# Filter features high over low on 128 partitions, and a differential head's values high beside low

## The chip, the cores and the metric

The kernel runs on one core of a Trainium2 chip. The metric is the device time of one execution in microseconds; the median of three runs stands for the kernel. The engines are TensorE (PE, with its weight loads as PEld), VectorE (DVE), ScalarE (ACT), GpSimd (POOL) and SyncE (SP), which issues most of the loads.

## The reference, cut to what matters

A residual stream of 256 tokens and 256 context tokens, 1024 wide, goes through a Hyena layer, an attention layer, and two trunk layers. Two places matter here. The first is the implicit filter of the Hyena layer, three sine layers of width 64 and a product with `w4`:

```python
    h = jnp.sin(fq * (z @ w1 + b1))
    h = jnp.sin(fq * (h @ w2 + b2))
    h = jnp.sin(fq * (h @ w3 + b3))
    h = h @ w4                       # (256, 2 * 2048)
    ...
    hf, hb = h[:, :E_HY] * decay, h[:, E_HY:] * decay
```

The second is the differential attention of the trunk layers, four heads of width 64 with two score maps each:

```python
    p = jax.nn.softmax(s, axis=-1)               # s: scores of the maps m = 0, 1
    a = p[:, :, 0] - lam * p[:, :, 1]
    return jnp.einsum('bhqk,bkhd->bqhd', a.astype(v.dtype), v)
```

The first trunk layer has 512 queries (256 of the context among them), the second 256.

## The kernel before, in words

Products are made in a rounded 32-bit form (`F32R`). To keep precision each factor is split into a high part and a low rest: `split` (L280) casts on ScalarE (L281) and subtracts on VectorE (L282). `mm3` (L284) then makes three matmuls, high by high, high by low, low by high (L285 to L287). Weights come by SP in blocks of 512 KB into five buffers and are split in the same way (`load_w`).

The filter. One load brings the weights of the sine layers, the positions `zt` and the biases (L493). Three sine layers follow on 64 partitions (L767 to L784): a matmul, the bias and the frequency (L776), a reduction of the argument (L778 to L782), the sine. Their result is split into `h3` (L787). `hy_filter` (L629) makes the filter of one of eight groups of 256 channels: it splits the group's `w4`, and for either parity of the positions one `mm3` with K = 64 gives 512 columns (L638), which VectorE multiplies by the decay (L640). The weights of group 0 are loaded by SP at the start, those of the others by ScalarE's queue (L624).

The differential attention. `keys` (L1145) splits the values into `vd`; `maps` (L1180) makes the scores of both maps, the exponentials and their weighted difference; `turn` transposes the result into `ats`; `values` (L1211) sums over the key tiles, two for the context queries and four for the others, with one `mm3` of 256 columns per tile. Its stationary operand is 128 columns wide, two heads, of which the unit uses one half: ScalarE copies that half to `od` (L1217). `attend` runs the three as a pipeline with lags. The sums and the transposes take turns in two PSUM banks (`tpps`, L262).

The order: in the first stage TensorE's instructions stand as written out (`START`, `manual_schedule`); elsewhere the order of each engine's instructions is worked out by the framework when the program is built. Each engine takes its instructions in order.

Of the kernel before, what the change touches and what calls it, by code (L numbers as in the profile page):

```python
# [15 lines left out]
F32 = mybir.dt.float32  # L16
# [6 lines left out]
P = 128  # L23
# [44 lines left out]
def _cols(v):  # L68

    return v.reshape(-1, P).T  # L70
# [10 lines left out]

def _vecs(i):

    z = [("ng0", _cols(i["norm_g"][0])), ("ab0", _cols(i["ada_b"][0])), ("ng1", _cols(i["norm_g"][1]))]
    for l in range(2):
        z += [(f"n1g{l}", _cols(i["norm1_g_2"][l])),
              (f"n2g{l}", _cols(i["norm2_g_2"][l]))]
    z.append(("fing", _cols(i["final_g_2"])))
    for l in range(2):
        z.append((f"ab{2 + l}", _cols(i["b_ada_2"][l])))  # L90
    z.append(("ab1", _cols(i["ada_b"][1])))
    for t in range(3):
        z.append((f"hcw{t}", _cols(i["hy_conv_w"][0, t])))
    z.append(("hcb", _cols(i["hy_conv_b"][0])))
    z.append(("hyd", _cols(i["hy_d"][0])))
    for l in range(2):
        for t in range(3):
            z.append((f"sc{l}{t}", _cols(i["sconv_w_2"][l, t])))
            z.append((f"fc{l}{t}", _cols(i["ffn_conv_w_2"][l, t])))
        z.append((f"sub{l}", np.tile(i["subln_g_2"][l], 2).reshape(P, 1)))  # L100
        for n in ("q1", "k1", "q2", "k2"):
            z.append((f"l{n}{l}", _rep(i[f"lambda_{n}_2"][l])))
    z += [("qg", _rep(i["at_q_g"][0])), ("kg", _rep(i["at_k_g"][0]))]
    off, o = {}, 0
    for n, v in z:
        off[n] = (o, v.shape[1])
        o += v.shape[1]
    return np.ascontiguousarray(np.concatenate([v for _, v in z], axis=1)), off
# [69 lines left out]
def _prep(i):  # L178
# [15 lines left out]

    A["ada3"] = np.ascontiguousarray(i["w_ada_2"][1].T.reshape(48, P, 1024))
    A["cbc"] = np.ascontiguousarray(np.broadcast_to(np.stack([i["c_2"][0], i["c_ctx_2"]])[None], (P, 2, 1024)))
    mlp = np.zeros((64, 3, 64), np.float32)
    mlp[:33, 0] = i["hy_fw1"][0]
    mlp[:, 1] = i["hy_fw2"][0]
    mlp[:, 2] = i["hy_fw3"][0]  # L200
    A["mlp"] = np.ascontiguousarray(np.concatenate(
        [mlp.reshape(64, 192), A.pop("t_z"), np.stack([i["hy_fb1"][0], i["hy_fb2"][0], i["hy_fb3"][0], i["hy_freq"][0]], 1)], 1))
    A["fw4"] = np.ascontiguousarray(i["hy_fw4"][0].reshape(64, 2, NG_HY, 256).transpose(2, 0, 1, 3))
    A["hy_in"] = _tile_w(i["hy_w_in"][0], 8, P)[:, 0]
    A["hy_out"] = _tile_w(i["hy_w_out"][0], 2, 512).transpose(1, 0, 2, 3, 4).copy()
    A["at_t"] = _tile_w(i["at_w_in"][0][:, :3072], 2, 512)
# [31 lines left out]
def _build(es, nc, tc, a, out, off, upto):  # L238
# [124 lines left out]

    def rsqrt(v, n, d, by=None):

        x = sm.tile([P, 16], F32, tag="rs_x", name="rs_x")[:, :n]
        r = sm.tile([P, 16], F32, tag="rs_r", name="rs_r")[:, :n]
        if by is None:
            V.tensor_scalar(x, v, 1.0 / d, EPS, op0=ALU.mult, op1=ALU.add)  # L369
        else:  # L370
            V.scalar_tensor_tensor(x, by, EPS, by, op0=ALU.mult, op1=ALU.mult)
            V.scalar_tensor_tensor(x, v, 1.0 / d, x, op0=ALU.mult, op1=ALU.add)
        G.tensor_tensor(r, x, mhalf[:, :n], op=ALU.pow)  # L373
        return r
# [114 lines left out]


    hp = es.enter_context(tc.tile_pool(name="hp", bufs=1))
    mlp_t = cst.tile([64, 452], F32, name="mlp")
    nc.sync.dma_start(mlp_t, a["mlp"])  # L493
    mlp = mlp_t[:, :192].rearrange("p (j c) -> p j c", j=3)
    zt, mlpb = mlp_t[:, 192:448], mlp_t[:, 448:]
    sc_c = cst.tile([P, 2, 8, 32], F32, name="sc_c")
    nc.sync.dma_start(sc_c, a["cvec"])
    S.activation(sc_c, sc_c, AF.Silu)
# [1 line left out]
    ident, ones64 = msk[:, :P], msk[:, P:P + 2]  # L500
    nv = a["vec"].shape[1]
    vec = cst.tile([P, nv], F32, name="vec")
    xt = cst.tile([P, 8, 512], F32, name="xt")
    ones128 = cst.tile([P, P], F32, name="ones128")
    V.memset(ones128, 1.0)
    mhalf = cst.tile([P, 16], F32, name="mhalf")
    V.memset(mhalf, -0.5)

    def vv(name):
# [104 lines left out]
    with ExitStack() as e1:  # L614
# [5 lines left out]
        mod_t = c1.tile([P, 4, 512], F32, tag="t_iv", name="mod_t")  # L620
        fw = _Pair(t_fw[:, 0], t_fw[:, 1])
        def hy_filter_load(g, q=nc.scalar, tmb=tmb):
            w4 = tmb()[:64]
            q.dma_start(w4, a["fw4"][g].rearrange("p b c -> p (b c)"))  # L624
            dec = tmb().rearrange("p (r c) -> p r c", r=2)
            q.dma_start(dec, a["t_dec"][g])
            return w4, dec

        def hy_filter(wd, tmp=tmb):  # L629

            w4, dec = wd
            w = pair(f1, [64, 512], "w4")
            split(w, w4)
            ep = pair(f1, [P, 2, 2, 256], "eo")
            sab = tmp(256)
            for par in range(2):
                ps = atps()
                mm3(ps, h3[:, par, :], w, True, True)  # L638
                kf = tmp().rearrange("p (b c) -> p b c", b=2)
                V.tensor_tensor(kf, ps.rearrange("p (b c) -> p b c", b=2),  # L640
                                dec[:, par, :].unsqueeze(1).to_broadcast([P, 2, 256]), op=ALU.mult)
# [117 lines left out]
        with tc.manual_schedule(engines={mybir.EngineType.PE}):  # L759
# [7 lines left out]
            for j in range(3):  # L767
                if j == 0:
                    nc.sync.dma_start(msk, a["t_m"])
                    nc.sync.dma_start(vec[:, :32], a["vec"][:, :32])  # L770
                    for k in range(0, 8, 4):
                        nc.sync.dma_start(xt[:, k:k + 4], a["x"][:, k:k + 4])
                ps = atps(256)
                T.matmul(ps[:64, :], mlp[:, j, :], hm, start=True, stop=True)
                ar = tmb(256)[:64]
                V.tensor_scalar(ar, ps[:64, :], mlpb[:, j:j + 1], mlpb[:, 3:4], op0=ALU.add, op1=ALU.mult)  # L776
                kk = tmb(256)[:64]
                V.tensor_scalar(kk, ar, 1.0 / two_pi, magic, op0=ALU.mult, op1=ALU.add)  # L778
                V.tensor_scalar(kk, kk, magic, None, op0=ALU.subtract)
                for pk in (p1, p2, p3):  # L780
                    V.scalar_tensor_tensor(ar, kk, -pk, ar, op0=ALU.mult, op1=ALU.add)
                V.tensor_scalar(ar, ar, 3.1415925, -3.1415925, op0=ALU.min, op1=ALU.max)  # L782
                hm = tmb(256)[:64]
                S.activation(hm, ar, AF.Sin)  # L784
                if j:
                    ada_step(2)
            h3 = pair(c1, [64, 2, P], "h3")  # L787
            split(h3, hm.rearrange("p (i r) -> p r i", r=2))
            f0 = hy_filter(wd)
            first, pb, done_k = [], [], []  # L790
            for what in START:
# [49 lines left out]
                else:  # L841
                    next(f0)
        filts = [x for x in f0 if x]
        nc.sync.dma_start(vec[:, 32:], a["vec"][:, 32:])
        t_iv = c1.tile([P, 2, 2, 2, 256], F32R, tag="t_iv", name="t_iv")
        G.dma_start(t_iv, a["t_iv"])
        iv = _Pair(t_iv[:, 0], t_iv[:, 1])
# [216 lines left out]
    for l in range(2):  # L1064
# [55 lines left out]
                    dst = ks[:, 4 * i:4 * i + 4, tok * P:tok * P + P]  # L1120
                S.copy(dst, tp[:96].rearrange("p (m t) -> p m t", m=4))

        vd = pair(a3, [P, 4, 256], "vd")
        gv = a3.tile([P, 4, 256], F32, tag="gv", name="gv")

        def diff_heads(ps, nm, tok):
# [17 lines left out]

        def keys(t, ps):  # L1145
            diff_heads(ps[:, :256], "k", t)
            split(vd[:, t, :], ps[:, 256:])

        def queries(t, ps):
            diff_heads(ps[:, 256:], "q", t)  # L1150
# [60 lines left out]
        def values(u):  # L1211
            i, sgm, b = blocks[u]
            k0, ns = (0, 4) if sgm == 0 else (2, 2)
            op = tpps()[:, :256] if ada_done[0] >= N_ADA else atps(256)
            for s in range(ns):
                mm3(op, vd[:, k0 + s, P * i:P * i + P], ats[u][:, s, :], s == 0, s == ns - 1)
            S.copy(od[64 * b:64 * b + 64, i, 256 * sgm:256 * sgm + 256], op[64 * b:64 * b + 64, :])  # L1217

        def attend(us):

# [212 lines left out]
```

## Time and profile before

| | us |
|---|---|
| median of 3 runs | 1822.44 (1822.36 to 1822.88) |
| profiled execution | 1825.12 |
| its span, first to last instruction | 1823.0 |
| TensorE busy | 1766.1 (97%) |
| VectorE busy | 1355.8 (74%) |
| ScalarE busy | 813.9 (45%) |
| mean granted TensorE clock | 0.987 |

Busy time of TensorE is made from matmul records that overlap, so that a busy share of 97% is no statement on how well the array is used; the distance between two starts is the time that a matmul takes from its successor. PEclk is the granted clock, 1.00 for 2.4 GHz and 0.50 for 1.2 GHz. In the rows, text in brackets is the idle time of the engine just before, and what ended it.

### The profile page before, as it was taken

What the parts mean: (1) busy time and instruction counts of PE and PEld (TensorE: products, weight loads), DVE (VectorE), ACT (ScalarE), POOL (GpSimd) and SP (SyncE); (2) the same over time, 40 slices, a digit from 0 to 9 for tenths busy, and PEclk for the clock granted to TensorE, in tenths of its full rate; (3) what the DMA queues carried; (4) which work ended last, traced back from release to release, by engine and by line L of the source; (5) the groups of instructions that cost most, each with busy time, mean ns of one, the idle gap of its engine ahead of it and who ended that gap; (6) DMA issues with size and microseconds to landing.
All of it is one profiled execution on the core that took longest, in us unless ns stands there. A gap on an engine that the chain in (4) does not pass through costs nothing.

```text
span 1823.0 us, 27469 instructions
## 1 busy us (share of the span) xinstructions
PE 1766.1 (97%) x10602; PEld 1483.5 (81%) x10602; DVE 1355.8 (74%) x2449; ACT 813.9 (45%) x1446; POOL 43.1 (2%) x42
## 2 busy tenths in 40 slices
PE   6999999999999999999999999999999998999998
PEld 2777788788777878889878889888888886889997
DVE  6778577577666776888878768887676877678786
ACT  3433233233333354656678426322322356455444
POOL 0000000000000010000000000000000000000000
PEclk9999999999999999999999999999999998999999
DMA  9454434444444344333442223545444633246562
GB/s 329 166 179 159 145 130 142 153 139 138 139 168 154 126 122 139 105 118 115 152 128 92 87 82 104 174 146 157 155 143 153 233 100 122 70 139 204 188 186 82
DMA packets 73889, 262.62 MB, mean 144 GB/s; under 512 B 8288, under 2 KB 9632, under 8 KB 73120
## 3 DMA queue, kind: packets, MB, share of 16 engines
q1 hardware_dynamic: 71328, 254.71, 43.1%
q10 hardware_dynamic: 1856, 3.28, 0.6%
q0 software_dynamic: 576, 2.88, 0.5%
q8 instruction: 84, 1.38, 0.3%
q14 instruction: 45, 0.37, 0.1%
HBM read 259.79 MB, written 1.05 MB: 143 GB/s over the span
## 4 chain that ended last, share of the span: by engine, by line
PE 87%; DVE 6%; ACT 2%; issue 1%; POOL 1%; DMA 1%; SPq 0%; POOLq 0%; DVEq 0%; ACTq 0%
PE mm L285 24%; PE mm L286 24%; PE mm L287 24%; PE at L285 3%; PE at L287 2%; PE at L286 2%; PE ad L525 2%; DVE wl L282 1%; POOL rs_r L373 1%; PE tp L995 1%; ACT wh L281 1%; DVE t L407 1%; PE tp L1208 1%; PE at L1191 1%; PE at L396 1%
## 5 line engine op out<-in xcount | busy, mean ns | idle before, releaser
L281 ACT CAST wh<-wr 128x1024 fp32r<-128x1024 f32 x328 | 342.9, 1050 | 572.4 <-PE mm L286 504.5
L285 PE MATMUL mm<-hh,wh 128*128 128x512 f32 (+1 forms) x1568 | 549.8, 352 | 2.4 <-ACT hh L422 1.1
L286 PE MATMUL mm<-hl,wh 128*128 128x512 f32 (+1 forms) x1568 | 546.0, 349 | 1.1 <-DVE hl L828 1.1
L282 DVE TENSOR_TENSOR wl<-wr,wh 128x1024 fp32r<-128x1024 f32 x328 | 399.3, 1220 | 198.1 <-ACT wh L281 197.5
L287 PE MATMUL mm<-hh,wl 128*128 128x512 f32 (+1 forms) x1568 | 544.5, 348 | 0.5 <-DVE wl L282 0.5
L285 PEld LDWEIGHTS mm<-hh,wh 128*128 128x128 f32 x1568 | 295.1, 189 | 56.5 <-issue 12.2
L287 PEld LDWEIGHTS mm<-hh,wl 128*128 128x128 f32 x1568 | 295.4, 189 | 40.0 <-DVE wl L282 0.9
L286 PEld LDWEIGHTS mm<-hl,wh 128*128 128x128 f32 x1568 | 295.5, 189 | 38.5 <-DVE hl L828 1.7
L487 DVE SCALAR_TENSOR_TENSOR xt<-mm,ada,xt 128x256 f32<-128x256 f32 x352 | 153.1, 477 | 28.9 <-PE mm L287 28.2
L285 PE MATMUL mm<-fh,wh 128*128 128x256 f32 (+1 forms) x384 | 124.4, 325 | 0.5 <-DVE xt L487 0.5
L286 PE MATMUL mm<-fl,wh 128*128 128x256 f32 (+1 forms) x384 | 124.5, 325 | 0.0
L287 PE MATMUL mm<-fh,wl 128*128 128x256 f32 (+1 forms) x384 | 124.3, 325 | 0.0
L586 DVE CUSTOM_DVE_ANT_0 junk<-av,cb,vec 128x1024 f32<-128x1024 f32 x64 | 82.0, 1281 | 27.1 <-DMA av<-in_ada_dram 26.6
L285 PE MATMUL mm<-wh,hh 128*128 128x512 f32 x240 | 96.3, 403 | 3.1 <-DVE t L904 2.3
L286 PE MATMUL mm<-wl,hh 128*128 128x512 f32 x240 | 95.7, 399 | 0.7 <-DVE wl L282 0.7
L287 PE MATMUL mm<-wh,hl 128*128 128x512 f32 x240 | 95.6, 398 | 0.0
L373 POOL TENSOR_TENSOR rs_r<-rs_x,mhalf 128x4 f32<-128x4 f32 (+2 forms) x34 | 40.6, 1194 | 1735.1 <-DVE rs_x L369 1629.6
L285 PEld LDWEIGHTS mm<-fh,wh 128*128 128x128 f32 x384 | 72.4, 189 | 7.4 <-DVE xt L487 0.7
L286 PEld LDWEIGHTS mm<-fl,wh 128*128 128x128 f32 x384 | 72.6, 189 | 6.7
L287 PEld LDWEIGHTS mm<-fh,wl 128*128 128x128 f32 x384 | 72.5, 189 | 6.6
L525 PE MATMUL ad<-ar,sc_c 128*32 128x256 f32 x768 | 57.1, 408 | 6.2 <-DMA ar<-in_ada_dram 6.1
L285 PE MATMUL mm<-ah,wh 128*128 128x512 f32 (+1 forms) x160 | 56.4, 354 | 0.0
(347 smaller groups left out, 2943.7 us busy)
## 6 DMA issues: line engine op xcount, KB each, us to landing
ar<-in_ada_dram SPq DMA_DIRECT2D x96, 512.0 KB, 4.4
wr<-in_w_u_dram SPq DMA_DIRECT2D x88, 512.0 KB, 3.9
wr<-in_hy_in_dram SPq DMA_DIRECT2D x64, 512.0 KB, 4.5
av<-in_ada_dram SPq DMA_DIRECT2D x48, 512.0 KB, 3.7
wr<-in_w_d_dram SPq DMA_DIRECT2D x44, 512.0 KB, 3.9
wr<-in_at_t_dram SPq DMA_DIRECT2D x24, 512.0 KB, 3.7
wr<-in_w_t_dram SPq DMA_DIRECT2D x24, 512.0 KB, 4.3
wr<-in_w_f_dram SPq DMA_DIRECT2D x20, 512.0 KB, 3.6
```

Of the source, the lines that this page charges most:

```text
L281: S.copy(dst.hi, src)
L282: V.tensor_tensor(dst.lo, src, dst.hi.bitcast(F32), op=ALU.subtract)
L285: T.matmul(ps, l.hi, r.hi, start=first, stop=False)
L286: T.matmul(ps, l.hi, r.lo, start=False, stop=False)
L287: T.matmul(ps, l.lo, r.hi, start=False, stop=last)
L373: G.tensor_tensor(r, x, mhalf[:, :n], op=ALU.pow)
L396: T.matmul(bc[:, t * P:(t + 1) * P], l, ident, start=True, stop=True)
L407: V.tensor_tensor(sqs[0], sqs[0], q, op=ALU.add)
L487: V.scalar_tensor_tensor(xt[:, m, c], ps[:, c], gts[j][:, m:m + 1], xt[:, m, c], op0=ALU.mult, op1=ALU.add)
L525: T.matmul(ps[32 * j:32 * j + 32, :], sc_c[:, l // 2, k, :], raw[:, 256 * j:256 * j + 256], start=(k == 0), stop=(k == 7), tile_position=( ...
L586: V.tensor_tensor_reduce(junk, raw, cb[:, v, :], 1.0, vv("ab3")[:, i:i + 1], op0=ALU.mult, op1=ALU.add, accum_out=ada[3][:, v, i:i + 1])
L995: T.transpose(tp[:, s * P:s * P + P], ps[hh, t][:, s * P:s * P + P], ident)
```

## The change

The features of the third sine layer are made twice, on 128 partitions (its weights stand twice side by side). `h3` then holds the high parts on partitions 0 to 63 and the low rests on 64 to 127, and `w4` is loaded twice, one copy under the other, and split as before. One matmul with K = 128 gives (high + low) by the high part of `w4`, a second one the same by its low part: two instead of three, and the product low by low is now in the sum. The biases move from the first load to the first four columns of `vec`, which get a load of their own.

In the differential attention `vd` holds 64 high columns and 64 low columns of each head side by side. A unit makes two matmuls per key tile, for the high and the low part of the map; rows 0 to 63 of the output then hold the sum with the high values, rows 64 to 127 the sum with the low ones. ScalarE copies rows 64 to 127 to a temporary, and VectorE adds both into `od`. The working tiles of `rsqrt` become 8 columns wide instead of 16, and the later parts of `vec` begin four columns further on.

```diff
--- before.py
+++ after.py
@@ -81,7 +81,8 @@
-    z = [("ng0", _cols(i["norm_g"][0])), ("ab0", _cols(i["ada_b"][0])), ("ng1", _cols(i["norm_g"][1]))]
+    z = [("fb", np.tile(np.stack([i[n][0] for n in ("hy_fb1", "hy_fb2", "hy_fb3", "hy_freq")], 1), (2, 1)))]
+    z += [("ng0", _cols(i["norm_g"][0])), ("ab0", _cols(i["ada_b"][0])), ("ng1", _cols(i["norm_g"][1]))]
@@ -194,13 +195,14 @@
-    mlp = np.zeros((64, 3, 64), np.float32)
+    mlp = np.zeros((64, 4, 64), np.float32)
     mlp[:33, 0] = i["hy_fw1"][0]
     mlp[:, 1] = i["hy_fw2"][0]
-    mlp[:, 2] = i["hy_fw3"][0]
-    A["mlp"] = np.ascontiguousarray(np.concatenate(
-        [mlp.reshape(64, 192), A.pop("t_z"), np.stack([i["hy_fb1"][0], i["hy_fb2"][0], i["hy_fb3"][0], i["hy_freq"][0]], 1)], 1))
-    A["fw4"] = np.ascontiguousarray(i["hy_fw4"][0].reshape(64, 2, NG_HY, 256).transpose(2, 0, 1, 3))
+    mlp[:, 2:] = i["hy_fw3"][0][:, None]
+    A["mlp"] = np.ascontiguousarray(np.concatenate([mlp.reshape(64, 256), A.pop("t_z")], 1))
+    fw4 = i["hy_fw4"][0].reshape(64, 2, NG_HY, 256).transpose(2, 0, 1, 3)
+    A["fw4"] = np.ascontiguousarray(np.concatenate([fw4, fw4], 1))
@@ -489,10 +491,9 @@
-    mlp_t = cst.tile([64, 452], F32, name="mlp")
+    mlp_t = cst.tile([64, 512], F32, name="mlp")
     nc.sync.dma_start(mlp_t, a["mlp"])
-    mlp = mlp_t[:, :192].rearrange("p (j c) -> p j c", j=3)
-    zt, mlpb = mlp_t[:, 192:448], mlp_t[:, 448:]
+    mlp, zt = mlp_t[:, :256], mlp_t[:, 256:]
@@ -500,10 +501,11 @@
     vec = cst.tile([P, nv], F32, name="vec")
+    nc.sync.dma_start(vec[:, :4], a["vec"][:, :4])
@@ -620,7 +622,7 @@
-            w4 = tmb()[:64]
+            w4 = tmb()
             q.dma_start(w4, a["fw4"][g].rearrange("p b c -> p (b c)"))
@@ -629,13 +631,14 @@
-            w = pair(f1, [64, 512], "w4")
+            w = pair(f1, [P, 512], "w4")
             split(w, w4)
...
                 ps = atps()
-                mm3(ps, h3[:, par, :], w, True, True)
+                for i, x in enumerate((w.hi, w.lo)):
+                    T.matmul(ps, h3[:, par, :], x, start=i == 0, stop=i == 1)
@@ -767,25 +770,30 @@
-                    nc.sync.dma_start(vec[:, :32], a["vec"][:, :32])
+                    nc.sync.dma_start(vec[:, 4:36], a["vec"][:, 4:36])
...
+                nr = P if j == 2 else 64
+                fb = vv("fb")[:nr]
                 ps = atps(256)
-                T.matmul(ps[:64, :], mlp[:, j, :], hm, start=True, stop=True)
-                ar = tmb(256)[:64]
-                V.tensor_scalar(ar, ps[:64, :], mlpb[:, j:j + 1], mlpb[:, 3:4], op0=ALU.add, op1=ALU.mult)
-                kk = tmb(256)[:64]
+                T.matmul(ps[:nr, :], mlp[:, 64 * j:64 * j + nr], hm, start=True, stop=True)
+                ar = tmb(256)[:nr]
+                V.tensor_scalar(ar, ps[:nr, :], fb[:, j:j + 1], fb[:, 3:4], op0=ALU.add, op1=ALU.mult)
+                kk = tmb(256)[:nr]
...
-                hm = tmb(256)[:64]
+                hm = tmb(256)[:nr]
                 S.activation(hm, ar, AF.Sin)
...
-            h3 = pair(c1, [64, 2, P], "h3")
-            split(h3, hm.rearrange("p (i r) -> p r i", r=2))
+            h3 = c1.tile([P, 2, P], F32R, name="h3")
+            hv = hm.rearrange("p (i r) -> p r i", r=2)
+            S.copy(h3, hv)
+            V.tensor_tensor(h3[64:], hv[64:], h3[64:].bitcast(F32), op=ALU.subtract)
@@ -1120,7 +1128,8 @@
-        vd = pair(a3, [P, 4, 256], "vd")
+        vd = a3.tile([P, 4, 4, 2, 64], F32R, tag="vd", name="vd")
@@ -1144,7 +1153,7 @@
             diff_heads(ps[:, :256], "k", t)
-            split(vd[:, t, :], ps[:, 256:])
+            split(_Pair(vd[:, t, :, 0, :], vd[:, t, :, 1, :]), ps[:, 256:].rearrange("p (h d) -> p h d", h=4))
@@ -1213,8 +1222,12 @@
             for s in range(ns):
-                mm3(op, vd[:, k0 + s, P * i:P * i + P], ats[u][:, s, :], s == 0, s == ns - 1)
-            S.copy(od[64 * b:64 * b + 64, i, 256 * sgm:256 * sgm + 256], op[64 * b:64 * b + 64, :])
+                v = vd[:, k0 + s, 2 * i + b].rearrange("p x d -> p (x d)")
+                T.matmul(op, v, ats[u].hi[:, s, :], start=s == 0, stop=False)
+                T.matmul(op, v, ats[u].lo[:, s, :], start=False, stop=s == ns - 1)
+            e = tmp(256)[:64]
+            S.copy(e, op[64:, :])
+            V.tensor_tensor(od[64 * b:64 * b + 64, i, 256 * sgm:256 * sgm + 256], op[:64, :], e, op=ALU.add)
```

## Rows read from the trace of the kernel before

**Rows 1.** The page, busy us and share of the span, by engine:
```profile
PE 1766.1 (97%) x10602; PEld 1483.5 (81%) x10602; DVE 1355.8 (74%) x2449; ACT 813.9 (45%) x1446; POOL 43.1 (2%) x42
```

**Rows 2.** The page, chain that ended last, by engine:
```profile
PE 87%; DVE 6%; ACT 2%; issue 1%; POOL 1%; DMA 1%; SPq 0%; POOLq 0%; DVEq 0%; ACTq 0%
```

**Rows 3.** Windows: us, busy PE, PEld, DVE, ACT, POOL (records), PEclk, DMA share, GB/s:
```profile
0.00:32.00 32.00, 16.07 (x105) 6.32 (x105) 18.98 (x52) 13.58 (x30) 2.30 (x7) 0.95 0.89 326
125.00:640.00 515.00, 515.00 (x2974) 409.94 (x2973) 350.38 (x597) 180.26 (x278) 0.71 (x1) 1.00 0.43 146
```

**Rows 4.** Filter weights' low half: duration ns min/median/max, first and last start us:
```profile
L286 PE MATMUL at<-w4l,h3h x16: 383/390/394, 50.4 to 559.6; 64*128 64x512 f32 x16
```

**Rows 5.** Timeline of TensorE in the first filter: start us, duration us:
```profile
50.61 0.39 PE L287 MATMUL at<-w4h,h3l 64*128 64x512 f32 x1
50.84 0.39 PE L285 MATMUL at<-w4h,h3h 64*128 64x512 f32 x1
```

**Rows 6.** DMA issues: queue, count, KB each, median us from issue to landing:
```profile
tb<-in_t_dec_dram ACTq DMA_DIRECT2D x7, 256.0 KB, 2.8
...
tb<-in_fw_dram ACTq DMA_DIRECT2D x7, 128.0 KB, 2.6
...
mlp<-in_mlp_dram SPq DMA_DIRECT2D x1, 113.0 KB, 2.8
...
vec<-in_vec_dram SPq DMA_DIRECT2D x1, 16.0 KB, 5.0
```

**Rows 7.** Timeline of TensorE, values of the first differential layer:
```profile
968.41 0.28 PE L287 MATMUL tp<-ath,vdl 128*128 128x256 f32 x1
968.53 0.28 PE L285 MATMUL tp<-ath,vdh 128*128 128x256 f32 x1
```

**Rows 8.** The tile of the heads' outputs, its copy from PSUM:
```profile
L1217 ACT COPY od<-tp x12: 353/367/368, 969.1 to 1566.2; 64x256 f32<-64x256 f32 x12
```

**Rows 9.** Groups by line and shape, a VectorE sum with one PSUM operand:
```profile
L717 DVE TENSOR_TENSOR t<-at,t 128x256 f32<-128x256 f32 x16 | 6.7, 417 | 0.0
```

**Rows 10.** Windows, the attention of the first differential layer:
```profile
960.00:1020.00 60.00, 59.98 (x329) 48.96 (x328) 53.77 (x132) 46.35 (x114) 2.01 (x2) 1.00 0.20 65
```

**Rows 11.** Waits from 960 to 1020: us in total, times, longest us:
```profile
PEld tp L1114 <- ACT od L1217: 0.3, 1, 0.3
```

**Rows 12.** Windows of the values' high half alone, second differential layer (no POOL):
```profile
1530.00:1562.00 32.00, 8.51 (x24) 6.42 (x24) 0.00 (x0) 0.00 (x0) 0.68 0.13 42
1562.00:1570.00 8.00, 1.72 (x8) 1.29 (x8) 0.00 (x0) 0.00 (x0) 1.00 0.00 0
```

**Rows 13.** Chain in order of time, one value step: start us, us:
```profile
1544.74 0.21 PE tp L287
```

**Rows 14.** Timeline behind the last matmul of a unit (idle before, releaser):
```profile
1546.91 0.36 ACT L1217 COPY od<-tp 64x256 f32<-64x256 f32 x1 [1.45 <-PE tp L287]
...
1548.19 0.69 DVE L1192 TENSOR_REDUCE dmx<-at 128x1 f32<-128x512 f32 x1 [2.14 <-PE at L1191]
```

**Rows 15.** Timeline of the start:
```profile
4.70 0.54 DVE L776 TENSOR_SCALAR tb<-at,mlp 64x256 f32<-64x256 f32 x1 [3.68 <-PE at L774]
...
5.91 1.32 DVE L781 SCALAR_TENSOR_TENSOR tb<-tb 64x256 f32<-64x256 f32 x3
...
7.89 0.62 ACT L281 CAST w4h<-tb 64x512 fp32r<-64x512 f32 x1 [0.49 <-DMA tb<-in_fw_dram]
...
9.15 0.28 DVE L782 TENSOR_SCALAR tb<-tb 64x256 f32<-64x256 f32 x1
```

**Rows 16.** Chain in order of time, a wait for modulation weights:
```profile
38.65 7.63 DMA ar<-in_ada_dram
```

**Rows 17.** Windows, granted clock in the second differential layer:
```profile
1530.00:1535.00 5.00, 3.21 (x19) 2.27 (x19) 4.10 (x11) 4.77 (x10) 1.82 (x1) 0.98 0.19 48
1535.00:1562.00 27.00, 20.73 (x77) 15.95 (x77) 20.95 (x47) 14.72 (x38) 0.00 (x0) 0.63 0.12 41
1546.00:1548.00 2.00, 2.00 (x11) 1.82 (x10) 0.05 (x1) 1.09 (x4) 0.00 (x0) 0.50 0.00 0
```

More of the change, by code (lines that the diff above doesn't have):

```diff
@@ L364, in rsqrt @@
     def rsqrt(v, n, d, by=None):
-        x = sm.tile([P, 16], F32, tag="rs_x", name="rs_x")[:, :n]
-        r = sm.tile([P, 16], F32, tag="rs_r", name="rs_r")[:, :n]
+        x = sm.tile([P, 8], F32, tag="rs_x", name="rs_x")[:, :n]
+        r = sm.tile([P, 8], F32, tag="rs_r", name="rs_r")[:, :n]
         if by is None:
@@ L505, in _build @@
     V.memset(ones128, 1.0)
-    mhalf = cst.tile([P, 16], F32, name="mhalf")
+    mhalf = cst.tile([P, 8], F32, name="mhalf")
     V.memset(mhalf, -0.5)
@@ L843, in _build @@
         filts = [x for x in f0 if x]
-        nc.sync.dma_start(vec[:, 32:], a["vec"][:, 32:])
+        nc.sync.dma_start(vec[:, 36:], a["vec"][:, 36:])
         t_iv = c1.tile([P, 2, 2, 2, 256], F32R, tag="t_iv", name="t_iv")
```

## The prediction

> **What bounds the kernel now.** I read the page first: its busy line, then the chain that ended last, then the windows, and only then the lines and tiles the change touches. The busy line [rows 1] has TensorE at work in 97% of the span and VectorE in 74%. The chain [rows 2] lies on TensorE for 87%, on VectorE for 6%. Windows [rows 3] show that this isn't even: in 125 to 640 us TensorE is busy in 515.00 of 515 us, while the first 32 us have it busy for half and the DMA engines for 0.89. Matmul records overlap, so I don't price a matmul by its duration but by the distance between two starts. So the reader should see three kinds of stretch: a start ruled by transfers and by short VectorE steps, a long middle in which every TensorE step costs its full distance, and two attention stages of the second block, the first of them (960 to 1020 us) with TensorE full, the second (1530 to 1562 us) with gaps and a lowered clock.
>
> **Filter: one matmul of three goes.** Per channel group and parity three matmuls of 512 columns become two, with 128 rows in place of 64. The removed kind has 16 instances, from 50.1 to 559.4 us [rows 4]; two neighbours start 0.23 us apart [rows 5]. More rows should not stretch the step: the 64-row step at 0.23 us has the same 512 columns as any other, and I take no change. 16 x 0.23 = 3.7 us, of which 14 instances lie where TensorE has no idle time or nearly none. The casts and subtractions of the weights keep their free size of 512 and so their time. The load of the weights, on ACT's queue from the second group on, doubles to 256 KB; loads of 128 and of 256 KB there take 2.6 and 2.8 us [rows 6], far ahead of use, so 0; without that cover 0.2 us a group. Gain 3.7 us; nothing else rules these stretches, so both ends are close (3.3 to 3.7).
>
> **Values of the first differential layer.** A unit (one head, one segment) had three matmuls of 256 columns per key tile and now has two: eight units, 4 x 2 + 4 x 4 = 24 steps fewer. Steps start 0.12 us apart [rows 7], so 2.8 us. Added to each unit: ScalarE's copy stays (it now goes to a temporary, 0.37 us, 12 in both layers [rows 8]), and behind it VectorE adds the other half in PSUM, for which the nearest row is a 128x256 sum with one PSUM operand, 0.42 us [rows 9]: 8 x 0.42 = 3.3 us. VectorE is busy 53.8 of the 60 us from 960 to 1020, TensorE 60.0 [rows 10]. After the change it would be 57.1 against 57.2: the addition fits only if VectorE never idles. Behind it on VectorE are maxima, weight splits and the subtractions that TensorE needs next. So the ends are 0 (VectorE takes all of it) and 2.8; I take 1.6, a little over half, because before the change VectorE's idle time here, 6.2 us, exceeds the 3.3 us added. The output bank is also held until the addition ends; this wait exists already, once, for 0.3 us [rows 11]. The temporary takes one more turn of the six-buffer ring; its neighbours in the ring are freed by the same engines, and I give it 0 beside the range.
>
> **Values of the second differential layer.** Four units with four key tiles: 16 steps fewer. From 1530 to 1562 the window of the tile has 24 matmuls that read the high half of the values, two of every three, so 36 steps or three units, at a mean granted clock of 0.68; the fourth unit lies behind, at 1.00 [rows 12]. On the chain the steps of the lowered clock, 1.2 GHz, are 0.21 us apart [rows 13]. 12 x 0.21 + 4 x 0.12 = 3.0 us, on the chain itself. Against it stands the addition: after the last matmul of a unit ScalarE copies from 1546.91, for 0.36 us, and VectorE has stood idle for 2.14 us when its next maximum begins at 1548.19 [rows 14]; there are three such gaps, one per unit. An addition of 0.42 us fits into them, but the next but one group of transposes wants the bank. If it waits for the addition, that is 0.42 us for each of three units, 1.3 us. If the addition also stands behind a maximum (0.69), four units lose 4.4 us, a net loss of 1.4. Ends: 3.0 gained and 1.4 lost; I take 2.0, nearer to the gap rows.
>
> **The start.** The biases and the frequency leave the first load and come by a load of their own, 128 rows of 16 bytes, third on SP's queue; all later loads there (weights, decay, mask, features, the modulation weights) are issued one step later. Before, the first step that needs a bias begins at 4.70 us, and its three reduction steps end at 7.23; VectorE then waits for the cast of the filter weights, which begins at 7.89 when their load lands, and clamps at 9.15 [rows 15]. The load of the first in line landed after 2.8 us, one of 128-byte rows further back after 5.0 [rows 6]; issued at about 2.0 us, the new one lands at 4.8 to 7.0. The later end moves the reductions to 9.5, and with the 0.64 us from the cast's end (8.51) to 9.15 behind them the clamp starts at 10.2, some 1.0 us late. At the earlier end only the doubled weight load shows, 0.2 us. Some 146 KB more at the 326 GB/s of this stretch [rows 3] add 0.45 us to what is behind them. What is late is late for all, since the chain goes from here over the steps of VectorE to the wait for modulation weights at 38.65 us [rows 16], whose transfer starts when TensorE frees a buffer. Cost 0.2 to 1.5 us; I take 0.9. The third layer's sine work runs on 128 partitions instead of 64 with the same free size, 0.
>
> The row of the 128-byte transfer, 5.0 us for 16 KB against 2.8 us for 113 KB, already looks like a price of short rows, or of its place in line [rows 6]. The Trainium skill, "DMA: Bandwidth & Descriptors", section "Specifications", speaks against this part of the change: a transfer wants at least 512 B for full rate, and below it does a read-modify-write. By that rule the later end would hold and the sum come out 0.5 us higher; by the rows alone both ends are open.
>
> **Sum.** -3.7 - 1.6 - 2.0 + 0.9 = -6.4 us. The profiled execution took 1825.12 us, with a span of 1823.0 and 2.1 us around it; it would become 1818.7. The median of the runs, 1822.44, lies 2.7 us below the profiled one, so I predict 1816.0. Best ends: -3.7 - 2.8 - 3.0 + 0.2 = -9.3, 1813.1. Worst: -3.3 + 0 + 1.4 + 1.5 = -0.4, 1822.0.
>
> **Rivals.**
> (1) VectorE becomes the bound. It takes the whole gain of the first layer and one bank wait per unit of the second: -3.7 - 0 - 1.7 + 0.9 = -4.5, or, with half of the rest lost too, -3.6: 1818 to 1819. For it: the 53.8 of 60 us. Against it: 6.2 us idle there.
> (2) The clock. In the second layer it is 0.98 until 1535, while TensorE is busy 3.21 of 5 us, 0.63 on the mean of 1535 to 1562, with stretches of 0.50 in which TensorE is fully busy (1546 to 1548) [rows 17], and 1.00 from 1562 on [rows 12]. Fewer matmuls between the same waits could leave it lower. A mean of 0.63 over 27 us means 7.0 us at 2.4 GHz and the rest at 1.2; TensorE is busy in 20.73 of the 27, so in about 5.4 of these 7.0 us, and needs 5.4 us more if all of it runs at 1.2 GHz. Result 1821.4. Against it: the clock rises and falls within the stage as it is, so it could as well come out better.
> [...]
> (3) Slower: the output bank. TensorE takes its instructions in order, and the transposes rotate over two banks with the value sums. If the new addition is put behind a weight split or a maximum on VectorE, each unit holds its bank for copy, queue and addition, and TensorE stands. The price per unit is up to 0.36 + 0.69 + 0.42, about 1.5 us, over 12 units 18 us; the gains apart from the units' waits are 3.7 + 2.8 + 3.0 - 0.9 = 8.6, so the kernel is slower from 0.7 us per unit on. At 1.1 us: 1822.4 - 8.6 + 13.2 = 1827.0. For it: the one wait on this copy that is there already [rows 11]. Against it: the idle 2.14 us [rows 14].
> (4) The change does not do what it says: the order of instructions is worked out anew when the program is built, and other places move. Where TensorE is full this costs nothing; around the start and the stage changes I allow 3 us either way, 1813 to 1819.
>
> **How the numbers follow.** About 0.2%, 3.6 us, is what a measurement here can tell from no change: faster is below 1818.8, slower above 1826.1. Forecast 0.63 (0.60 faster, 0.03 same); rival 1, 0.13 (0.05, 0.08); rival 2, 0.10 (0.02 faster, 0.08 same); rival 3, 0.09 (0.02 same, 0.07 slower); rival 4, 0.05 (0.03, 0.02). Together faster 0.70, same 0.23, slower 0.07. The range 1812 to 1822 holds the forecast with its bounds, and rivals 1, 2 and 4 nearly whole; rival 3 is left out.
>
> **What would show it.** Filter: two matmul records per parity, 32 in all, still 0.23 us apart, and the stretch up to the first block's end shorter by 3.7 us less the start's loss. First layer: TensorE still full in the stage and VectorE above 93%. If TensorE has gaps there that end with VectorE, rival 1 holds. Second layer: the addition right behind the copy, and 8 steps per unit after which transposes follow without a gap; a gap that ends with the addition is rival 3. The granted clock of this stage tells rival 2. Start: the first bias step between 4.7 and 7.1 us. I would be wrong most likely in how much of the 5.8 us of both value stages is kept, and in the start.

## The result, and the profile after

| | before | after |
|---|---|---|
| median of the runs, us | 1822.4 | 1832.6 (1832.0 to 1835.7) |
| ratio, with its 95% interval | | 1.0051 (1.0035 to 1.0066) |
| profiled execution, its span | 1825.1, 1823.0 | 1832.2, 1829.6 |

The kernel became 10.2 us slower by the medians, 9.3 by the ratio; forecast were 6.4 us less, and the range ended at 1822. The page of after, its busy line and its chain (for rows 1 and 2):

```profile
PE 1770.2 (97%) x10546; PEld 1487.5 (81%) x10546; DVE 1361.6 (74%) x2461; ACT 815.2 (45%) x1446; POOL 43.5 (2%) x42
...
PE 86%; DVE 6%; ACT 3%; issue 2%; POOL 2%; DMA 1%; POOLq 0%; DVEq 0%; SPq 0%; ACTq 0%
```

There are 56 matmuls fewer (as forecast: 16, 24 and 16), and yet TensorE is busy 4.1 us longer. So the loss isn't only waiting: steps that are left must have become longer, by a lower clock or otherwise. Next come the windows that answer to rows 10 and 17, with the columns of rows 3:

```profile
960.00:1020.00 60.00, 57.11 (x291) 44.61 (x290) 52.56 (x129) 44.08 (x102) 2.43 (x2) 1.00 0.20 58
1535.00:1562.00 27.00, 21.11 (x68) 14.57 (x67) 21.00 (x47) 14.22 (x37) 0.00 (x0) 0.50 0.08 24
```

The first differential layer had TensorE full, 59.98 us [rows 10]; now it has gaps, though VectorE is less busy than before, 52.56 against 53.77. TensorE's longest wait there is for ScalarE's exponential (960 to 1025 us, before and then after; us in total, times, longest):

```profile
PEld at L1191 <- ACT t L1194: 1.1, 5, 0.3
PEld at L1200 <- ACT t L1203: 4.1, 9, 1.2
```

The second ran at a mean granted clock of 0.63 [rows 17]; now it is 0.50 throughout, the lower level.

Where the time went is read from the starts of those VectorE, ScalarE and GpSimd instructions that both traces have. How far after lies behind before, at the end of each stretch, and in brackets what the stretch added:

| up to, us | after behind before, us |
|---|---|
| 45 | +1.0 (+1.0) |
| 125 | -1.9 (-2.9) |
| 640 | -5.7 (-3.8) |
| 960 | -3.2 (+2.5) |
| 1040 | -1.1 (+2.1) |
| 1530 | -1.1 (0) |
| 1575 | +2.9 (+4.0) |
| 1823 | +6.6 (+3.7) |

The other 3.6 us of the 10.2 don't show between these two traces: before's profiled execution was itself 2.7 us above its median. About 1.4 us of that lie in the first 60 us, where two kernels below with the same start are ahead of it by 1.2 (e3_shift) and 2.4 us (e2_values). And 1.9 of the +2.5 up to 960 us go with a drop of the granted clock near 920 us in this one execution of after; in e4_unshift (below), with the same instructions, such drops stand near 864 and 939 us instead, so that I count their place as chance. So four things are left to explain: a gain in the filters as forecast, a loss in either differential layer, and a loss of 3.7 us at the end, where the change touches nothing.

### The profile page after: what moved, and what is told of

Read it like the earlier page. It is cut to its first block, busy times and chain, and to the rows that moved or that the text cites. A ratio compares the mean times of both kernels' runs of the same rounds, so it can differ in the third digit from the quotient of the medians.

```text
span 1829.6 us, 27376 instructions
## 1 busy us (share of the span) xinstructions
PE 1770.2 (97%) x10546; PEld 1487.5 (81%) x10546; DVE 1361.6 (74%) x2461; ACT 815.2 (45%) x1446; POOL 43.5 (2%) x42
## 4 chain that ended last, share of the span: by engine, by line
PE 86%; DVE 6%; ACT 3%; issue 2%; POOL 2%; DMA 1%; POOLq 0%; DVEq 0%; SPq 0%; ACTq 0%
PE mm L287 24%; PE mm L288 24%; PE mm L289 24%; PE ad L527 2%; PE at L287 2%; PE at L288 2%; PE at L289 2%; POOL rs_r L375 2%; DVE wl L284 1%; PE tp L1003 1%; ACT wh L283 1%; DMA ar<-in_ada_dram 1%; PE at L1200 1%; PE at L398 1%; PE at L385 0%
## 5 line engine op out<-in xcount | busy, mean ns | idle before, releaser
L287 PEld LDWEIGHTS mm<-wh,hh 128*128 128x128 f32 x240 | 45.4, 190 | 13.3 <-ACT t L909 1.2
```

The source lines that it names most:

```text
L287: T.matmul(ps, l.hi, r.hi, start=first, stop=False)
```

## The experiments

**Theories.** (A) The parts act alone: the filter part gains, and the values lose through VectorE's addition and the output bank. (B) A part that the prediction didn't cost: new tile sizes move the weight tiles in SBUF, and this sets the pace of steps that are otherwise the same. (C) The clock: fewer matmuls leave it low in the second layer. (D) The temporary's turn in the six-buffer ring, given 0 in the prediction.

All ratios are against runs of before on the same chip, taken together with the kernel; one thousandth is 1.8 us.

### e1_filter and e2_values: the two halves apart

e1 is after with the `vd`, `keys` and `values` of before (the lines that differ from after):

```diff
-        vd = a3.tile([P, 4, 4, 2, 64], F32R, tag="vd", name="vd")
+        vd = pair(a3, [P, 4, 256], "vd")
...
-            split(_Pair(vd[:, t, :, 0, :], vd[:, t, :, 1, :]), ps[:, 256:].rearrange("p (h d) -> p h d", h=4))
+            split(vd[:, t, :], ps[:, 256:])
...
+                mm3(op, vd[:, k0 + s, P * i:P * i + P], ats[u][:, s, :], s == 0, s == ns - 1)
+            S.copy(od[64 * b:64 * b + 64, i, 256 * sgm:256 * sgm + 256], op[64 * b:64 * b + 64, :])
```

and e2 is before with those of after, the same lines the other way round. e2 leaves all weight tiles where they were.

> The filter part alone on the kernel before: features high over low, weights twice, biases in their own load, and the new tile sizes (which move the weight tiles by 192 bytes in each partition); the attention as before. From the two traces the stretch of the filters became 4.0 us shorter, and the first 45 us about 0.9 us longer. If these two are all that the part does: 1822.4 - 4.0 + 0.9 = 1819.3 us. If the 256-column steps with weights as the stationary operand pace by where the weight tiles lie (117 ns before, 120 ns after, in 690 to 900 and 1640 to 1800 us), 3.0 to 4.5 us more: 1822.3 to 1823.8 us. If the drop of the granted clock near 920 us belongs to the filter part, another 1.9 us.

> The values of the differential attention alone on the kernel before: high beside low, two matmuls per key tile, the copy of one half and the addition of the other; all tiles of the weights where they were. If the attention stages lose by themselves what the trace of after shows there (2.1 us in the first layer, 4.0 to 5.3 in the second): 1822.4 + 6.1 to 7.4 = 1828.5 to 1829.8 us. If they lose only together with the filter part, through an order of instructions or a clock that the filter part shifts: 1818.8 (the 3.6 us of the prediction) to 1822.4 us.

Measured: e1 1.0010 (1.0001 to 1.0019), so +1.8 us; e2 1.0037 (1.0023 to 1.0052), +6.7. The half that should gain 2.8 us loses 1.8, and the values lose in both layers without the filter part.

### e3_shift and e4_unshift: only addresses

e3 is before with

```diff
-        x = sm.tile([P, 16], F32, tag="rs_x", name="rs_x")[:, :n]
-        r = sm.tile([P, 16], F32, tag="rs_r", name="rs_r")[:, :n]
+        x = sm.tile([P, 8], F32, tag="rs_x", name="rs_x")[:, :n]
+        r = sm.tile([P, 8], F32, tag="rs_r", name="rs_r")[:, :n]
...
-    mhalf = cst.tile([P, 16], F32, name="mhalf")
+    mhalf = cst.tile([P, 64], F32, name="mhalf")
```

e4 is after with

```diff
-    ada = [cst.tile([P, 2, n], F32, name=f"ada{l}") for l, n in enumerate(ada_nt)]
+    ada = [(cst if l else sm).tile([P, 2, n], F32, name=f"ada{l}", bufs=1) for l, n in enumerate(ada_nt)]
```

Each has the instructions of its parent in the same order. In before and e4 the first high weight tile begins at byte 64160 of each partition, in after and e3 at 64352; `h` begins at 118464 in all.

> The kernel before, instruction for instruction, with one tile of constants longer and the two working tiles of rsqrt 8 columns wide, so that the raw weights and their high and low parts lie 192 bytes further on in each partition, as they do in after; nothing else moves but these working tiles. If the place of the weight tiles sets the pace: 256-column steps of 120 ns in place of 117 in 690 to 900 and 1640 to 1800 us, and 3.0 to 4.5 us more than before, 1825.4 to 1826.9 us. If the pace is a matter of the single run or of the rest of the change: 117 ns, and 1822.4 us within 1 us.

> The kernel after, instruction for instruction, with the modulation of the first layer (192 bytes) behind the weight tiles instead of ahead of them, so that all weight tiles lie where they lay before. If their place sets the pace: 117 ns in place of 120, and 3.0 to 4.5 us less than after, 1828.1 to 1829.6 us. If not: 1832.6 us within 1 us.

Measured: e3 1.0035 (1.0023 to 1.0048), +6.4 us, without any change in what is computed; e4 1.0010 (1.0001 to 1.0018), 7.5 us less than after. More than expected, but B holds. Groups by line and shape show it without any window: matmuls of 256 columns in before, then in e3 (count, then busy us and mean ns):

```profile
L285 PE MATMUL mm<-hh,wh 128*128 128x256 f32 x656 | 183.6, 282 | 1.1 <-ACT hh L422 1.1
L286 PE MATMUL mm<-hl,wh 128*128 128x256 f32 x656 | 183.2, 281 | 0.0
```

```profile
L285 PE MATMUL mm<-hh,wh 128*128 128x256 f32 x656 | 186.0, 286 | 1.1 <-ACT hh L422 1.1
L286 PE MATMUL mm<-hl,wh 128*128 128x256 f32 x656 | 185.4, 284 | 0.0
```

And the window from 1640 to 1800 us, before and then e3, both at a clock of 1.00 and without gaps worth the name:

```profile
1640.00:1800.00 160.00, 159.54 (x1360) 159.34 (x1360) 130.64 (x211) 80.23 (x119) 0.00 (x0) 1.00 0.59 183
```

```profile
1640.00:1800.00 160.00, 160.00 (x1342) 160.00 (x1341) 130.13 (x211) 82.06 (x119) 0.00 (x0) 1.00 0.61 188
```

In the same time e3 gets 18 matmuls less done. From start to start such a step takes 116.7 to 117.6 ns in before and 119.8 to 120.2 in e3, by stretch; with 1968 of them (three kinds of 656) some 3.1 ns each are 6.1 us, close to the measured 6.4. Steps of 512 columns keep their 0.23 us.

### e8_places: the pace by the two addresses alone

Behind the end of before, 100 groups of 24 matmuls of 256 columns (2400 in all), with both operands in tiles of their own at offsets in steps of 32 bytes, and nothing else running:

```python
                    w = wm[:, ow + 4096 * iw + 128 * k:][:, :128]
                    x = hm[:, oh + 4096 * ih + 512 * k:][:, :256]
                    T.matmul(ps, w, x, start=k == 0 and iw + ih == 0, stop=k == 7 and iw == 1)
```

> The kernel before, and behind its end 100 groups of 24 matmuls of 256 columns as in its projections, with nothing else running: weights and moving operand from two tiles of their own, at byte offsets that go through one stretch of 512 bytes in steps of 32, first of the weights, then of the moving operand (once with the weights at the offset that they have before within 512 bytes, once at that of after). If the pace follows from the two addresses alone: some 116.7 ns a step at the pair of offsets of before, 120 ns at that of after, and other values at others. If it takes other engines' accesses: one value, near 117 ns or below, for all offsets.

Two windows of its one execution, each cut at the starts of the first of 48 matmuls and of the first behind them (the counts take in those that reach over an edge): the pair of offsets of before (weights at 160 of 512 bytes, moving operand at 192), then that of after (352 and 192):

```profile
1996.17:2001.83 5.66, 5.66 (x50) 5.66 (x49) 0.00 (x0) 0.00 (x0) 0.00 (x0) 1.00 0.01 3
2087.22:2092.97 5.75, 5.75 (x51) 5.75 (x49) 0.00 (x0) 0.00 (x0) 0.00 (x0) 1.00 0.01 3
```

From start to start that is 117.9 and 119.7 ns a step, with VectorE, ScalarE and GpSimd idle. So 1.8 of the kernel's 3.1 ns come without any other engine; where the other 1.3 come from isn't shown. Over the whole sweep the pace goes by the address of the moving operand less that of the weights, modulo 256 bytes: 119.7 to 120.0 ns at 0 and 96, 118.5 to 118.7 at 128 and 160, 118.2 to 118.4 at 224, 117.7 to 118.0 at 32, 64 and 192. For `h` and the weights the change moved it from 32 to 96, from the best class into the worst. Two other moving operands of the kernel, which lie at the same addresses in before and e3, agree: for `og` it goes from 32 to 96 too, and the step from 116.7 to 119.9 ns; for `a` (`ah` and `al` in the rows) it goes from 96 to 160, and the step gets shorter, from 120.0 to 118.2 (some 190 steps each). Three pairs fall out of the pattern: with the moving operand at 320 and the weights at 160 or 416 it is 117.3 to 117.4 where 118.6 was due, and with 352 and 160, in one block of 48, 113.7; why stays open. The pattern is that of these traces and of this shape (128 weight columns, 256 moving columns); no other was swept.

### e5_noadd and e6_refill: the addition, or the missing matmuls

Both stand on e4. e5 leaves the addition out, and with it the part of the sums that comes from the low values:

```diff
-            e = tmp(256)[:64]
-            S.copy(e, op[64:, :])
-            V.tensor_tensor(od[64 * b:64 * b + 64, i, 256 * sgm:256 * sgm + 256], op[:64, :], e, op=ALU.add)
+            S.copy(od[64 * b:64 * b + 64, i, 256 * sgm:256 * sgm + 256], op[:64, :])
```

e6 keeps the addition and puts the number of matmuls back:

```diff
+            for s in range(ns):
+                T.matmul(op, vd[:, k0 + s, 2 * i + b].rearrange("p x d -> p (x d)"), ats[u].hi[:, s, :], start=True, stop=True)
             for s in range(ns):
```

> As e4_unshift, but the halves aren't added: ScalarE copies rows 0 to 63 straight into the heads' output, and the temporary and VectorE's addition are left out (the part of the sums that comes from the low values is left out of the result). The matmuls stay two per key tile. e4_unshift loses 2.1 us between 960 and 1040 us and 3.8 us between 1530 and 1575 us against before. If the addition causes both (VectorE's time, the bank held longer, the copy and the addition at the end of the stage): no loss left, and a gain between 0 and 2.8 us in the first stage and between 0 and 3.0 us in the second, 5 to 10 us less than e4_unshift. If the missing matmuls cause it (TensorE isn't the bound in either stage, the order is made anew, and fewer matmuls leave the clock of the second stage at 0.62 in place of 0.74): the second stage still loses 2 to 4 us and the first is within 1 us of before; 2 to 3 us less than e4_unshift.

> As e4_unshift, with the number of matmuls of before: ahead of each unit's sum one more matmul per key tile, whose result the sum overwrites (24 in the first differential layer, 16 in the second); the addition stays. If TensorE bounds the stages: 24 x 0.12 + 16 x 0.12 to 0.21, 4.8 to 6.2 us more than e4_unshift. If the clock of the second stage falls because matmuls are missing there: the mean granted clock of 1530 to 1570 us back from 0.62 to 0.74 or more, and the stage no longer than in e4_unshift. If VectorE and ScalarE bound the first stage: 960 to 1040 us as long as in e4_unshift within 0.5 us, though 2.9 us of matmuls are added.

Measured: e5 0.9948 (0.9930 to 0.9967), 11.3 us less than e4. e6 1.0004 (0.9990 to 1.0019): with 40 matmuls more, no slower than e4. Windows of the second layer for e4, e5 and e6, in this order:

```profile
1530.00:1570.00 40.00, 29.12 (x110) 21.27 (x110) 26.85 (x60) 20.31 (x50) 1.41 (x2) 0.62 0.10 34
```

```profile
1530.00:1570.00 40.00, 34.51 (x207) 29.34 (x208) 28.02 (x64) 22.35 (x53) 2.01 (x2) 0.79 0.09 27
```

```profile
1530.00:1570.00 40.00, 29.55 (x144) 23.39 (x144) 27.37 (x63) 20.60 (x51) 2.50 (x3) 0.74 0.11 33
```

C falls as the cause: e5 has as few matmuls as e4 and the highest clock of the three, with TensorE busy 34.51 us of the 40 against 29.12. As an amplifier it is likely but not shown: e6 has 0.74 with matmuls that do nothing, and its trace loses 1.9 us less than e4's between 1530 and 1575 us. But e1's trace, with the values of before, is 1.9 us shorter there than before's, so one trace can differ by that much without a cause in the kernel. Over all runs the mean granted clock of the whole execution is 0.986 for e6 and 0.984 for e4 (10 and 11 runs). In the first layer e6 loses 1.6 us more than e4 up to 1040 us (with 2.9 us of matmuls added), at a clock of 1.00 in both.

### e7_filter_unshift

e1 with the line of `ada` of e4.

> The filter part alone, as e1_filter, with the modulation of the first layer behind the weight tiles, so that these lie where they lay before. If the place of the weight tiles and the two terms of the filter part (4.0 us less in the filters, 0.9 us more in the start) are independent: 3 to 4 us less than before. If the place only matters together with other parts: as e1_filter, 1 to 3 us more than before.

Measured: 0.9977 (0.9967 to 0.9988), 4.2 us less than before and 6.0 less than e1. The place and the filter part add up.

### e9_own_tile, e10_gpsimd, e11_sbuf_add: what of the addition costs

e9 is e4 with

```diff
-            e = tmp(256)[:64]
+            e = a3.tile([P, 256], F32, tag="e", name="e", bufs=2)[:64]
```

e10 copies both halves out of PSUM and adds in SBUF; e11 is e10 with `V` in place of `G`:

```diff
+            o = od[64 * b:64 * b + 64, i, 256 * sgm:256 * sgm + 256]
+            e = a3.tile([P, 256], F32, tag="e", name="e", bufs=2)[64 * b:64 * b + 64]
+            S.copy(o, op[:64, :])
+            S.copy(e, op[64:, :])
+            G.tensor_tensor(o, o, e, op=ALU.add)
```

> As e4_unshift, but the temporary of the values lies in two buffers of its own and no longer takes a turn of the six-buffer ring, in which the exponentials lie too. e5_noadd, without temporary and addition, was 11 us less than e4_unshift. If the turn of the ring is what costs (an exponential waits for the buffer that the addition still reads): most of the 11 us come back, 8 to 11 us less than e4_unshift. If it is the addition (VectorE's time, the output bank held until it ends): e4_unshift within 2 us.

> As e9_own_tile, but ScalarE copies both halves out of PSUM (0.37 us each in place of one copy), and GpSimd, busy 2% of the span, adds them in SBUF. If VectorE's time and the bank held for the addition cost the 11 us: ScalarE's second copy holds the bank as long as the addition did (0.37 for 0.42 us), but VectorE is free: 5 to 9 us less than e4_unshift. If the ring alone costs: as e9_own_tile within 1 us. If it is the length of the hold: as e4_unshift within 2 us.

> As e10_gpsimd, but VectorE adds the halves in SBUF, after ScalarE's two copies. The bank is then freed by ScalarE, and VectorE has the same additional work as in e4_unshift. If the bank's wait for VectorE's queue costs: 5 to 9 us less than e4_unshift. If VectorE's time costs: e4_unshift within 2 us, while e10_gpsimd is faster.

Measured: e9 0.9972 (0.9960 to 0.9985), 6.9 us less than e4; e10 0.9996 (0.9984 to 1.0008); e11 0.9980 (0.9970 to 0.9990). So D holds for 6.9 of the 11.3 us, by another buffer for the temporary alone in the text of the kernel; the addition itself keeps 4.4 (e9 against e5). Taking it off VectorE doesn't help: GpSimd needs 887 ns for one (12 in its trace), and e11, which frees the bank by two copies of ScalarE, isn't better than e9 either.

What the ring does is seen on ScalarE. Before, in the second layer (start, us, what; in brackets the idle time ahead and what ended it):

```profile
1544.68 0.69 ACT L1194 ACTIVATE t<-at,dmx 128x512 f32<-128x512 f32 x1 [1.00 <-DVE dmx L1192]
...
1546.91 0.36 ACT L1217 COPY od<-tp 64x256 f32<-64x256 f32 x1 [1.45 <-PE tp L287]
```

The same place in after:

```profile
1545.01 0.37 ACT L1229 COPY t<-tp 64x256 f32<-64x256 f32 x1 [2.43 <-PE tp L1227]
1545.41 0.69 ACT L1203 ACTIVATE t<-at,dmx 128x512 f32<-128x512 f32 x1
...
1546.24 0.80 PE L1200 MATMUL at<-ks,qs 96*128 96x512 f32 x1 [0.46 <-ACT t L1203]
```

And in e9:

```profile
1541.41 0.69 ACT L1203 ACTIVATE t<-at,dmx 128x512 f32<-128x512 f32 x1 [1.00 <-DVE dmx L1201]
...
1542.79 0.37 ACT L1229 COPY e<-tp 64x256 f32<-64x256 f32 x1 [0.59 <-PE tp L1227]
```

Before and in e9 an exponential of the next unit runs ahead of the copy, while TensorE still makes the unit's sum. In after the copy stands first, ScalarE idles 2.43 us until the sum is done, the exponential starts behind it, and TensorE waits for that with its next scores, at the lower clock. The waits of 1528 to 1570 us, after and then e9 (us in total, times, longest):

```profile
PEld at L1200 <- ACT t L1203: 9.5, 12, 2.0
ACT t L1229 <- PE tp L1227: 9.2, 4, 2.4
```

```profile
PEld at L1200 <- ACT t L1203: 7.1, 9, 2.0
...
ACT e L1229 <- PE tp L1227: 2.8, 2, 2.2
```

The granted clock goes along. From 1530 to 1570 us it is 0.62 in e4 (above); in e9:

```profile
1530.00:1570.00 40.00, 31.82 (x170) 25.92 (x171) 29.40 (x65) 23.00 (x54) 2.49 (x3) 0.74 0.10 34
```

In the built program of this layer the temporary keeps one of the ring's six buffers for three of the four units, and the exponentials go round in the other five. How much of the 6.9 us is the buffer's turn itself, the order that the framework makes from it, or the clock wasn't separated.

### e12_second_layer: what is worth keeping

e9 with the three matmuls of before in the first layer; two and the addition in the second.

```diff
+            if l == 0:
+                for s in range(ns):
+                    mm3(op, vd[:, k0 + s, P * i:P * i + P], ats[u][:, s, :], s == 0, s == ns - 1)
+                S.copy(od[64 * b:64 * b + 64, i, 256 * sgm:256 * sgm + 256], op[64 * b:64 * b + 64, :])
+                return
```

> As e9_own_tile (filter part, weight tiles where they lay before, temporary of its own), but the first differential layer has the three matmuls and the copy of before; only the second has the two matmuls and the addition. From the traces: the first layer cost e9_own_tile 1.8 us against before (from -5.0 at 960 us to -3.2 at 1040 us), which should go; the second gave it 2.8 us, which should stay. If the layers are independent: 1.8 us less than e9_own_tile and 2.8 us less than e7_filter_unshift, 6 to 8 us less than before. If the gain of the second layer hangs on where the clock falls within it: between e7_filter_unshift (4 us less than before) and 7 us less.

Measured: 0.9966 (0.9953 to 0.9979), 6.2 us less than before, the fastest of those that compute the whole result, if not clearly apart from e9 and e7. In its trace the first layer costs nothing against before, and 1530 to 1575 us are 3.2 us shorter, of which up to 1.9 can be chance, as e1's trace shows.

## Why the prediction was wrong, step by step

The parts, as ratios between neighbouring kernels in us, beside the terms of the sum:

| part | forecast | measured | from |
|---|---|---|---|
| filter with the start | -3.7 + 0.9 | -4.2 | e7 against before |
| 40 value matmuls less | -5.8 | -5.3 | e5 against e7 |
| the addition itself | +2.2 | +4.4 | e9 against e5 |
| the temporary in the ring | 0 | +6.9 | e4 against e9 |
| weight tiles 192 bytes on | not in the sum | +7.5 (6.0 to 7.5) | after against e4; e3 against before 6.4; e1 against e7 6.0 |

The parts lie one upon the other, so that they sum to after's +9.3 us by construction; each is uncertain by 2 to 4 us (by 4 where e5, with four runs, is in it).

**The place of the weight tiles** is the first step that failed, and it failed by not being there. The prediction followed every instruction that the change adds or removes, but not the sizes of the tiles: `mlp` is 60 columns longer, `vec` four, and `mhalf` has 8 in place of 16. These lie ahead of the weight tiles, which so move by 192 bytes; the shorter tiles of `rsqrt` lie behind them and make up for it, so that everything further on stays. That the steps between keep their pace was taken for granted; e3 shows that they don't.

The Trainium skill, "SBUF — State Buffer", section "SBUF: two separate sides", says of the engines that only a port pair shared by VectorE and GpSimd makes them wait, and that TensorE never waits for anyone. The runs don't speak against that: in e8_places the other engines are idle, and the pace still goes by TensorE's own two addresses, by 1.8 ns between the two pairs shown.

**The ring** is the second: "The temporary takes one more turn of the six-buffer ring; its neighbours in the ring are freed by the same engines, and I give it 0 beside the range." Who frees a buffer was the wrong question. The buffer's turn came with another order on ScalarE, in which a copy that waits 2.4 us stands ahead of the exponential that TensorE needs next. Rival 4 had the order in view, but bounded it with 3 us.

**The addition** came out at 4.4 in place of 2.2, but with an uncertainty of some 4 us, so that its size isn't shown to be wrong. In the first layer I let VectorE take it in its idle 6.2 us [rows 10]. e9's trace loses 1.8 us there against before, where e5's, without it, gains 2.5. A part can be the clock: from 960 to 1040 us it is 0.98 on the mean in e9 and 1.00 in e5, and 0.04 of 80 us at half the pace would be 1.6 us (an estimate). Rival 3 had the sign right, but for a reason that carries little of it: it asked for 1.1 us of waits for the bank in each of 12 units, and in the second layer of e9 the transposes wait for the addition once, for 0.8 us. What the rest of the 4.4 us is made of wasn't separated.

**The matmuls** were right within that uncertainty: the 5.8 us as an upper end when nothing is added against 5.3 measured, and e5's first layer is full again (79.82 of 80 us from 960 to 1040).

**The filter** gained more than 3.7. One group before, and then after (start and duration, us):

```profile
320.00 0.40 PE L287 MATMUL mm<-hh,wl 128*128 128x512 f32 x1
320.32 0.50 PE L285 MATMUL at<-w4h,h3h 64*128 64x512 f32 x1
320.66 0.39 PE L286 MATMUL at<-w4l,h3h 64*128 64x512 f32 x1
320.90 0.39 PE L287 MATMUL at<-w4h,h3l 64*128 64x512 f32 x1
...
321.90 0.64 PE L525 MATMUL ad<-ar,sc_c 128*32 128x256 f32 x8
```

```profile
317.03 0.39 PE L289 MATMUL mm<-hh,wl 128*128 128x512 f32 x1
317.26 0.40 PE L641 MATMUL at<-w4h,h 128*128 128x512 f32 x1
317.50 0.39 PE L641 MATMUL at<-w4l,h 128*128 128x512 f32 x1
...
318.28 1.07 PE L527 MATMUL ad<-ar,sc_c 128*32 128x256 f32 x16
```

From the last matmul ahead of the group to the first behind it: 1.90 us before, 1.25 after, 0.65 in place of two times 0.23. The distances of 0.32 and 0.34 where 128 rows change to 64 are 0.23 and 0.24 when both have 128. The rows beside rows 5 would have shown it; I read the middle of a group only. (The first and last starts in rows 4 are 50.4 and 559.6 us, not the prediction's 50.1 and 559.4; nothing hangs on it.) Eight groups at 0.65 are 5.2, less 1.0 of the start: the measured 4.2. The Trainium skill, "TensorEngine Tiling (Array Packing)", section "Key Properties", has it that a change of the tiling mode drains the engine. The trace agrees in that the first step on 64 rows starts 0.09 us late; the second, as late again, needs no change of mode, and whether either is a drain isn't shown.

**The start** was right. The new load, issued at 2.00 us, lands 4.7 us later, near the later of the two ends, and the first step that needs a bias waits for it (the view of the DMA issues, then the timeline):

```profile
vec<-in_vec_dram SPq DMA_DIRECT2D x1, 2.0 KB, 4.7
```

```profile
6.83 0.54 DVE L781 TENSOR_SCALAR tb<-at,vec 64x256 f32<-64x256 f32 x1 [5.81 <-DMA vec<-in_vec_dram]
```

It began at 4.70 before [rows 15]. At 45 us after is 1.0 us behind; 0.9 were taken.

**Rival 2** (the clock) had its sign: 0.50 throughout in after. But it asked for fewer matmuls as the cause, and e5, with as few, ran at 0.79; in these traces the clock went with the waits. **Rival 1** doesn't hold: VectorE's share fell where it should have risen, and most of TensorE's wait in the first layer is for ScalarE (4.1 us).

## What to carry to other kernels

A change of a tile's size is a change of every address behind it: put the operands' addresses beside the diff, and pad until the tiles of the main loop lie where they lay, before a part is judged. A temporary for a step off the critical path wants buffers of its own where the ring it would join carries the tiles of the next unit (here 6.9 us). And price a removed matmul with its neighbours: the distances on both sides of a group belong to it.

## What the runs showed of the hardware that was not expected

- The pace of matmuls of 256 columns goes by the addresses of their operands modulo 256 bytes: 117.7 to 120.0 ns (e8_places, nothing else running; three pairs apart); in the kernel 117 against 120, and e3_shift, with 1968 such steps, 6.4 us slower.
- A group of matmuls on 64 rows among others on 128 costs about 0.1 us more at its first and at its second step (0.32 and 0.34 us in place of 0.23).
- Matmuls that do nothing can come at no cost in time: e6_refill ran 40 more than e4_unshift in no more time, with the granted clock of the second layer at 0.74 in place of 0.62 in its trace.
